# Value units of a conv-MLP kernel: sums formed half a group ahead, and the next group's first block product between a unit's last two

## The chip, the cores and the metric

The kernel runs on one core of a Trainium2 chip (trn2). The metric is the device time in microseconds of one execution; lower is better. Before the change, three runs took 1213.5, 1215.37 and 1215.85 us: a median of 1215.37.

## The reference, cut to what matters

A causal decoder trunk of two layers for 512 tokens of width 1024, all in float32. Layer 0 mixes tokens by sliding-window attention and a short convolution, layer 1 by gated linear attention. After its mixer each layer has the gated MLP with a causal convolution of width 3 that this change is about, and then a per-layer embedding:

```
def _conv_ffn(h, w_up, conv_w, conv_b, w_down):
    u = _causal_depthwise_conv(h @ w_up, conv_w) + conv_b
    gate, up = jnp.split(u, 2, axis=-1)
    return (jax.nn.gelu(gate, approximate=False) * up) @ w_down
...
x = x + _conv_ffn(_rms_norm(x, ffn_norm[i]), ffn_w_up[i], ffn_conv_w[i], ffn_conv_b[i], ffn_w_down[i])
```

`w_up` is 1024 x 5632: 2816 gate columns and 2816 value columns, in 22 blocks of 128 each (`NF` = 22).

## The kernel before, in words

**Precision.** A float32 product is done as three faster fp32r products. Each operand is cut into a rounded part and a remainder: ScalarE copies it to the rounded type (`wh`, line 870 in the `ffn`), VectorE subtracts (`wl`, line 873), and TensorE adds hi x hi, hi x lo and lo x hi (lines 924 to 926, three matmuls of 128 x 256 each per piece). `cut_into` and `cut_blocks` (lines 854 to 876) do one such cut; ScalarE's half is listed in the trace as an ACTIVATE of line 870, VectorE's as a TENSOR_TENSOR of line 873.

**Seven block products.** A pair of column blocks (256 columns) times the 512 tokens is a 2 x 2 block product, and `seven` (lines 928 to 956) does it with seven products of 12 matmuls instead of eight. The tokens' side has the forms e1, o1, o2, s1 to s4; the weights' side has `plain` (blocks as they are), `t13` (two sums of blocks), `t2` (one more combination) and `last` (a remainder of the odd rows, cut late at line 951). The order is: W = plain x e1 in a bank of its own; W copied to the left halves of X and Y (lines 940 and 941); V = t13 x s1 beside W; X left += plain x o1; Y left += t2 x s2; Y left copied to X right (line 950); X right += t13 x s3, copied to Y right (line 953); Y left += last x s4; X right += last x o2. It is a generator: the caller takes it step by step and puts other products between the steps.

**Groups.** `ffn` (from line 960) runs over eleven groups d of a gate pair and the two value blocks that come after it. A gate pair is always done by `seven`. The values are done as full products of 24 matmuls (`value`), but in groups 1 and 4 (`pairs_by_blocks`) by a `Unit` (lines 1062 to 1095), which does a value pair in the same seven products, between the gate's steps. TensorE's order is written out by hand (main loop from line 1195): `first` (the unit's W) comes after the gate's Y left; `second` (V, X left, Y left, then the cut of `last`) after the gate's X right; `third` (X right s3) after the gate's last product; then `begin` for the next group, which for a unit is the next gate's W, and `fourth` (Y left s4, X right o2). The order on the other engines comes from a scheduler, which the code steers with `tc.issue_after(instruction)` and `tc.high_priority(offset)`.

**Sums.** `sum_ahead` (line 1022) has the DMA engines form the sums of weight blocks that make `t13`: one 512 KB transfer from GpSimd's queue (line 1028), and when it has landed two accumulating transfers of 256 KB (line 1030). It is used for the gate pairs of groups 1, 2 and 3, and for the two units. `sum_forms` (line 1034) then cuts them. For a unit (`apart`) it cuts `plain`, cuts the sums into a tile `four` (the trace shows `four<-four` at line 870), forms b11 (line 1042), cuts it as t2 and forms b21 (line 1045). A unit's sums were asked for as early as the scheduler would take them.

**Loads.** Gate weights are loaded by SyncE (line 1108), values too (line 1001), 1 MB each, into two `raw` buffers. A buffer is free when VectorE has done `last`'s remainder. `prepare(d)` (lines 1097 to 1118) issues the sums and loads of group d and the cuts that follow; it is called at the end of group d - 1, with `copied`, that group's copy at line 953.

VectorE and ScalarE also run the convolution taps of every group (lines 978 to 990), the gelu (line 1245) and the product of gate and value (line 1138). In the trace, a matmul whose right operand is listed as `four,wh` is one with the sums of token forms.

Of the kernel before, what the change touches and what calls it, by code (L numbers as in the profile page):

```python
# [19 lines left out]
P = 128  # L20
# [4 lines left out]
DFF = 2816  # L25
# [35 lines left out]
HALVES = (slice(0, S // 2), slice(S // 2, S))  # L61


class Kernel:
# [860 lines left out]
            mm(out, wh, xl, start=False, stop=False, **kw)  # L925
            mm(out, wl, xh, start=False, stop=j == ND // 2 - 1, **kw)  # L926

    def seven(self, od, ws, x, keep=None):


        nc = self.nc
        H = S // 2
        product = self.block_product
        left, right = HALVES
        W = self.pa()
        V = W[:, right]
        X, Y = self.ps(), self.ps()
        plain, t13, t2 = ws
        product(W[:, left], plain, 0, x["e1"], True)
        nc.scalar.copy(X[:, left], W[:, left])  # L940
        nc.scalar.copy(Y[:, left], W[:, left])
        yield
        product(V, t13, 0, x["s1"])
        more = V
        if keep is not None:
            more = keep()
            nc.scalar.copy(more, V)
        product(X[:, left], plain, 1, x["o1"])
        product(Y[:, left], t2, 0, x["s2"])
        yield nc.scalar.copy(X[:, right], Y[:, left])  # L950
        last = self.cut_blocks(od)
        product(X[:, right], t13, 1, x["s3"])
        yield nc.scalar.copy(Y[:, right], X[:, right])
        product(Y[:, left], last, 1, x["s4"])
        product(X[:, right], last, 0, x["o2"])
        yield X, Y, more

    def ffn(self, i, project, next_gain):


        nc, a, tc = self.nc, self.a, self.tc
        gain = self.g_ffn[i]
        wu = a["ffn_w_up"][i].rearrange("(k p) n -> p k n", p=P)
        w0, w1, w2, bb = self.fcv

        mine, other = (("a0", "a1"), ("b0", "b1"))[:: 1 - 2 * i]
        with tc.tile_pool(name=f"ffn{i}", bufs=1) as fp:
# [27 lines left out]
            def load_values(d):  # L995

                c0, c1 = DFF + 256 * d + P, min(DFF + 256 * d + 3 * P, 2 * DFF)
                if d < 0:
                    c0 = DFF
                raw = self.raw(ND, 256)[:, :, : c1 - c0]  # L1000
                nc.sync.dma_start(raw, wu[:, :, c0:c1])
                return raw

            def column(raw, c):
                return self.cut(raw[:, :, c * P : (c + 1) * P], "b", BLOCKS)
# [11 lines left out]
            pairs_by_blocks = (1, 4)  # L1017
            ahead_of = {0: (1, 2), 1: (3,)}
            blocks = a["ffn_w_up"][i].rearrange("(j u p) n -> u p j n", p=P, u=2)
            gate_sums, value_sums, places = {}, {}, {}  # L1020

            def sum_ahead(sums, d, c):
                key = id(sums)
                if key not in places:
                    x = self.four(fp, F32).rearrange("p (h a) b -> p h (a b)", h=2)
                    places[key] = [x[:, h].rearrange("p (j n) -> p j n", n=2 * P) for h in range(2)]
                x = sums[d] = places[key][d % 2 if sums is gate_sums else 0]
                nc.gpsimd.dma_start(x, blocks[0, :, :, c : c + 2 * P])
                for u in range(2):
                    nc.gpsimd.dma_start(  # L1030
                        x[:, :, u * P : (u + 1) * P], blocks[u, :, :, c + P : c + 2 * P], accum_op=ALU.add
                    )

            def sum_forms(raw, both13, apart=False):
                ev, od = self.by_parity(raw)
                if apart:
                    b11, b21, b22 = ev[:, :, :P], od[:, :, :P], od[:, :, P:]
                    plain = self.cut_blocks(raw[:, :, :P])
                    four = self.four(fp)
                    h, l = (four[:, 2 * u : 2 * u + 2].rearrange("p a b -> p (a b)") for u in range(2))  # L1040
                    t13 = self.cut_into(h, l, both13)
                    nc.vector.tensor_tensor(b11, b22, both13[:, :, :P], ALU.add)
                    with tc.high_priority(offset=40):
                        t2 = self.cut_blocks(b11, False)
                    nc.vector.tensor_tensor(b21, b21, b11, ALU.add)
                    return plain, t13, t2
                plain = self.cut_blocks(raw[:, :, :P])
                given = both13 is not None
                if not given:
                    both13 = ev  # L1050
                first, third = both13[:, :, :P], both13[:, :, P:]
                if not given:
                    nc.vector.tensor_tensor(first, ev[:, :, P:], ev[:, :, :P], ALU.add)
                    nc.vector.tensor_tensor(third, od[:, :, P:], ev[:, :, P:], ALU.add)  # L1054
                t13 = self.cut_blocks(both13)
                nc.vector.tensor_tensor(first, od[:, :, P:], first, ALU.add)
                with tc.high_priority(offset=40):
                    t2 = self.cut_blocks(first, False)
                nc.vector.tensor_tensor(od[:, :, :P], od[:, :, :P], first, ALU.add)
                return plain, t13, t2  # L1060

            class Unit:
# [22 lines left out]
                    u.last = self.cut_blocks(u.od)  # L1085

                def third(u):
                    right = HALVES[1]
                    self.block_product(u.X[:, right], u.t13, 1, operands["s3"])
                    nc.scalar.copy(u.Y[:, right], u.X[:, right])  # L1090

                def fourth(u):
                    left, right = HALVES
                    self.block_product(u.Y[:, left], u.last, 1, operands["s4"])
                    self.block_product(u.X[:, right], u.last, 0, operands["o2"])

            def prepare(d, behind=None):

                if d == 0:
                    values.append(load_values(-1))  # L1100
                rv, w0 = values.pop(), None
                if d - 1 not in pairs_by_blocks:
                    with tc.issue_after(behind.ins) if behind else nullcontext():
                        w0 = column(rv, rv.shape[2] // P - 1)
                if d in pairs_by_blocks:
                    sum_ahead(value_sums, d, DFF + 256 * d + P)
                rg = self.raw(ND, 256)
                nc.sync.dma_start(rg, wu[:, :, 256 * d : 256 * d + 256])
                ev, od = self.by_parity(rg)
                ws = sum_forms(rg, gate_sums.get(d))  # L1110
                values.append(load_values(d))
                steps = self.seven(od, ws, operands, self.aside)
                for e in ahead_of.get(d, ()):
                    sum_ahead(gate_sums, e, 256 * e)
                if d not in pairs_by_blocks:
                    return steps, w0, column(values[0], 0)
                rv = values[0]
                return steps, w0, Unit(rv, sum_forms(rv, value_sums[d], True))

            def begin(d, steps, w):  # L1120

# [71 lines left out]
            operands = self.tokens_and_forms(xg, self.forms)  # L1193
            ready = []

            def done(m, ps):
                nc.vector.tensor_tensor(self.xT[m], self.xT[m], ps, ALU.add)
                self.operand(m, gain, mine)

            project(done, lambda: ready.extend(prepare(0)))  # L1200
            steps, w0c, w1c = ready
            with tc.manual_schedule(engines={ET.PE}):
                late = begin(0, steps, w0c)
                close = lambda: None
                for d in range(groups):
# [4 lines left out]
                    unit = w1c if isinstance(w1c, Unit) else None  # L1210
# [17 lines left out]
                    if d + 1 < groups:  # L1228
                        steps, w0c, w1c = prepare(d + 1, copied)
                        if unit:  # L1230
                            unit.third()
                            w0c = unit
                        else:
                            cut = self.rest_cut
                        late = begin(d + 1, steps, w0c)
                    else:
                        split_acts()
# [1174 lines left out]
```

## Time and profile before

| what | value |
|---|---|
| median of three runs | 1215.37 us |
| profiled execution | 1216.1 us |
| its span, first to last instruction | 1214.3 us |
| its mean granted TensorE clock | 0.995 |
| TensorE busy | 1192.9 us, 98% |
| VectorE busy | 1001.8 us, 83% |
| ScalarE busy | 701.5 us, 58% |

The profiled execution's own time is 1.8 us above its span, which is what lies around the first and the last instruction. Waits are written behind a row of the timeline in brackets: the idle time in us ahead of the instruction, and what released it. `PE ... [1.85 <-ACT wh L870]` says that TensorE stood for 1.85 us until ScalarE's rounding of line 870 was done. A row begins with its start (us from the span's start) and its length. In the windows, the column behind the five engines is the granted clock of TensorE.

The two MLPs lie at 178 to 440 us (layer 0) and 803 to 1085 us (layer 1). Their units are in groups 1 and 4: at about 204 to 239 and 273 to 302, and at 830 to 862 and 898 to 925.

### The profile page before, as it was taken

To read this page: it belongs to the slowest core of one execution; us is meant where nothing else is said; L and a number is where in the kernel's file an instruction comes from. 1 tells how busy PE (TensorE), PEld (TensorE's weight loads), DVE (VectorE), ACT (ScalarE), POOL (GpSimd) and SP (SyncE) were. 2 spreads that over 40 slices of the span, in tenths; PEclk is the share of its full clock that TensorE was granted. 3 is DMA by queue.
4 is the path that set the end of the run, shared out by engine and by line. 5 is a ranking of instruction groups with operands and counts; after the bars stand their busy time and mean duration, and the time that the engine had idled before them with its cause. 6 is when DMAs were issued, how large, how long until landed. Compare 5 with 4: busy or idle time off the path is not lost.

```text
span 1214.3 us, 20267 instructions
## 1 busy us (share of the span) xinstructions
PE 1192.9 (98%) x8170; PEld 1080.3 (89%) x8170; DVE 1001.8 (83%) x1603; ACT 701.5 (58%) x1166; POOL 80.0 (7%) x94
## 2 busy tenths in 40 slices
PE   9999999899999999999999999999999999999998
PEld 8887789898999989989988988899999999888887
DVE  6786688698999996789879876687898999988595
ACT  7466556455556654666674655555565556646374
POOL 3600211100000000000100002012000000000000
PEclk9999999899999999999999999999999999999999
DMA  7222553542333343322412215345323242433501
GB/s 220 84 92 70 127 126 100 125 136 70 106 104 107 120 134 100 105 77 80 148 59 67 87 56 134 92 129 159 95 83 127 71 139 75 145 103 96 206 2 70
DMA packets 125074, 128.26 MB, mean 106 GB/s; under 512 B 3336, under 2 KB 118722, under 8 KB 124980
## 3 DMA queue, kind: packets, MB, share of 16 engines
q1 hardware_dynamic: 112144, 115.88, 29.7%
q0 software_dynamic: 12560, 10.91, 5.0%
q8 instruction: 64, 1.05, 0.4%
q14 instruction: 30, 0.25, 0.1%
q10 hardware_dynamic: 276, 0.18, 0.0%
HBM read 124.86 MB, written 2.10 MB: 105 GB/s over the span
## 4 chain that ended last, share of the span: by engine, by line
PE 72%; DVE 12%; DMA 6%; issue 6%; ACT 4%; POOL 1%; ACTq 0%; POOLq 0%; DVEq 0%; SPq 0%
PE ps L177 8%; PE ps L178 8%; PE ps L179 7%; PE ps L193 4%; PE ps L191 4%; DMA four<-in_ffn_w_up_dram 4%; PE ps L200 4%; PE ps L924 4%; PE ps L926 4%; PE ps L925 4%; PE pa L178 3%; PE pa L179 3%; PE pa L177 3%; DVE wl L873 3%; DVE zt L990 2%
## 5 line engine op out<-in xcount | busy, mean ns | idle before, releaser
L153 DVE TENSOR_TENSOR wl<-raw,wh 128x1024 fp32r<-128x1024 f32 (+3 forms) x130 | 149.2, 1150 | 36.3 <-ACT wh L151 33.7
L151 ACT ACTIVATE wh<-raw 128x1024 fp32r<-128x1024 f32 (+4 forms) x134 | 132.5, 991 | 69.2 <-PE ps L178 26.9
L870 ACT ACTIVATE wh<-raw 128x1024 fp32r<-128x1024 f32 x92 | 97.7, 1062 | 116.1 <-DVE raw L1054 42.3
L873 DVE TENSOR_TENSOR wl<-raw,wh 128x1024 fp32r<-128x1024 f32 x92 | 112.6, 1224 | 34.3 <-ACT wh L870 33.2
L990 DVE SCALAR_TENSOR_TENSOR zt<-z,vfa,zt 128x511 f32<-128x511 f32 (+1 forms) x176 | 129.9, 747 | 1.6 <-ACT zt L988 1.1
L988 ACT ACTIVATE zt<-z,vfb 128x512 f32<-128x512 f32 x88 | 70.5, 812 | 31.4 <-DVE z L978 13.9
L179 PE MATMUL pa<-b,wl 128*128 128x256 f32 x288 | 79.7, 277 | 0.1
L179 PE MATMUL pa<-a,wl 128*128 128x256 f32 x288 | 79.6, 276 | 0.0
L177 PE MATMUL pa<-b,wh 128*128 128x256 f32 x288 | 79.5, 276 | 0.0
L178 PE MATMUL pa<-b,wh 128*128 128x256 f32 x288 | 79.5, 276 | 0.0
L177 PE MATMUL pa<-a,wh 128*128 128x256 f32 x288 | 79.5, 276 | 0.0
L178 PE MATMUL pa<-a,wh 128*128 128x256 f32 x288 | 79.5, 276 | 0.0
L191 PE MATMUL ps<-b,wh 128*128 128x512 f32 (+1 forms) x192 | 72.9, 383 | 0.0
L193 PE MATMUL ps<-b,wh 128*128 128x512 f32 (+1 forms) x192 | 72.2, 379 | 0.0
L924 PE MATMUL ps<-four,wh 128*128 128x256 f32 x232 | 64.9, 280 | 1.0 <-ACT ps L950 1.0
L926 PE MATMUL ps<-four,wl 128*128 128x256 f32 x232 | 64.1, 276 | 0.0
L925 PE MATMUL ps<-four,wh 128*128 128x256 f32 x232 | 64.1, 276 | 0.0
L179 PEld LDWEIGHTS pa<-b,wl 128*128 128x128 f32 x288 | 54.1, 188 | 0.3 <-DVE wl L153 0.2
L177 PEld LDWEIGHTS pa<-b,wh 128*128 128x128 f32 x288 | 54.1, 188 | 0.0
L178 PEld LDWEIGHTS pa<-b,wh 128*128 128x128 f32 x288 | 54.1, 188 | 0.0
L177 PEld LDWEIGHTS pa<-a,wh 128*128 128x128 f32 x288 | 54.1, 188 | 0.0
L178 PEld LDWEIGHTS pa<-a,wh 128*128 128x128 f32 x288 | 54.1, 188 | 0.0
(564 smaller groups left out, 3947.2 us busy)
## 6 DMA issues: line engine op xcount, KB each, us to landing
raw<-in_ffn_w_up_dram SPq DMA_DIRECT2D x42, 1024.0 KB, 5.0
raw<-in_ffn_w_down_dram SPq DMA_DIRECT2D x13, 1024.0 KB, 5.2
raw<-in_hy_w_in_dram SPq DMA_DIRECT2D x8, 1024.0 KB, 5.2
raw<-in_gla_w_in_dram SPq DMA_DIRECT2D x8, 1024.0 KB, 5.1
raw<-in_ffn_w_down_dram SPq DMA_DIRECT2D x8, 768.0 KB, 4.9
raw<-in_ple_w_gate_dram SPq DMA_DIRECT2D x6, 1024.0 KB, 5.4
four<-in_ffn_w_up_dram POOLq DMA_DIRECT2D x10, 512.0 KB, 4.6
four<-in_ffn_w_up_dram POOLq DMA_DIRECT2D x20, 256.0 KB, 6.6
```

The source lines that it names most:

```text
L151: nc.scalar.activation(hv, v, AF.Copy)
L153: self.rest_cut = nc.vector.tensor_tensor(lv, v, hv.bitcast(F32), ALU.subtract)
L177: mm(out, lh, rh, start=start, stop=False, **kw)
L178: mm(out, lh, rl, start=False, stop=False, **kw)
L179: mm(out, ll, rh, start=False, stop=stop, **kw)
L191: mm(out, lh, rh, start=first, stop=False, **kw)
L193: end = mm(out, lt, rt, start=False, stop=False, **kw)
L873: nc.vector.tensor_tensor(l, src, h.bitcast(F32), ALU.subtract)
L924: mm(out, wh, xh, start=first and j == 0, stop=False, **kw)
L925: mm(out, wh, xl, start=False, stop=False, **kw)
L926: mm(out, wl, xh, start=False, stop=j == ND // 2 - 1, **kw)
L990: nc.vector.scalar_tensor_tensor(out=y[:, tap:], in0=z[:, : S - tap], scalar=w[:, f : f + 1], in1=y[:, tap:], op0=ALU.mult, op1=ALU.add,)
```

## The change

It has four parts. Line numbers of the changed kernel are one higher than those above from line 928 on, and up to five higher behind line 1110.

1. The sums of a unit are issued after the `copied` instruction of the group before. Their first transfer is issued from ScalarE's queue instead of GpSimd's; the two accumulating ones stay on GpSimd's.
2. The cut of these sums into `t13` is issued after the same instruction.
3. `third` now does X right s3, the copy of X right to Y right, and Y left s4. `fourth` does X right o2 alone. The next gate's W thus stands between the unit's last two products instead of ahead of both.
4. In a unit's group, the gate's `last` cut has a priority that is higher by 100.

```diff
-    def seven(self, od, ws, x, keep=None):
+    def seven(self, od, ws, x, keep=None, sooner=0):
...
-        last = self.cut_blocks(od)
+        with self.tc.high_priority(offset=sooner) if sooner else nullcontext():
+            last = self.cut_blocks(od)
...
-            def sum_ahead(sums, d, c):
+            def sum_ahead(sums, d, c, q=nc.gpsimd):
...
-                nc.gpsimd.dma_start(x, blocks[0, :, :, c : c + 2 * P])
+                q.dma_start(x, blocks[0, :, :, c : c + 2 * P])
...
-            def sum_forms(raw, both13, apart=False):
+            def sum_forms(raw, both13, behind=None):
...
-                    t13 = self.cut_into(h, l, both13)
+                    with tc.issue_after(behind.ins):
+                        t13 = self.cut_into(h, l, both13)
...
                 def third(u):
-                    right = HALVES[1]
+                    left, right = HALVES
                     self.block_product(u.X[:, right], u.t13, 1, operands["s3"])
                     nc.scalar.copy(u.Y[:, right], u.X[:, right])
 
+                    self.block_product(u.Y[:, left], u.last, 1, operands["s4"])
+
                 def fourth(u):
-                    left, right = HALVES
-                    self.block_product(u.Y[:, left], u.last, 1, operands["s4"])
+                    right = HALVES[1]
                     self.block_product(u.X[:, right], u.last, 0, operands["o2"])
...
                 if d in pairs_by_blocks:
-                    sum_ahead(value_sums, d, DFF + 256 * d + P)
+                    with tc.issue_after(behind.ins):
+                        sum_ahead(value_sums, d, DFF + 256 * d + P, nc.scalar)
...
-                steps = self.seven(od, ws, operands, self.aside)
+                unit = d in pairs_by_blocks
+                steps = self.seven(od, ws, operands, self.aside, 100 if unit else 0)
...
-                return steps, w0, Unit(rv, sum_forms(rv, value_sums[d], True))
+                return steps, w0, Unit(rv, sum_forms(rv, value_sums[d], behind))
```

More of the change, by code (lines that the diff above doesn't have):

```diff
@@ L1032, in sum_ahead @@
                     )
-            def sum_forms(raw, both13, apart=False):
+            def sum_forms(raw, both13, behind=None):
                 ev, od = self.by_parity(raw)
-                if apart:
+                if behind:
                     b11, b21, b22 = ev[:, :, :P], od[:, :, :P], od[:, :, P:]
@@ L1111, in prepare @@
                 values.append(load_values(d))
-                steps = self.seven(od, ws, operands, self.aside)
+                unit = d in pairs_by_blocks
+                steps = self.seven(od, ws, operands, self.aside, 100 if unit else 0)
                 for e in ahead_of.get(d, ()):
                     sum_ahead(gate_sums, e, 256 * e)
-                if d not in pairs_by_blocks:
+                if not unit:
                     return steps, w0, column(values[0], 0)
                 rv = values[0]
-                return steps, w0, Unit(rv, sum_forms(rv, value_sums[d], True))
+                return steps, w0, Unit(rv, sum_forms(rv, value_sums[d], behind))
             def begin(d, steps, w):
```

## The prediction

> **What bounds the kernel now.** I read the head of the page first, then TensorE's waits by line, then the timeline of TensorE around the four units (groups 1 and 4 of each layer), and last ScalarE's timeline and the DMA queues there. Page and waits (engine, tile, line, waited for; total us, times, longest):
>
> ```profile
> span 1214.3 us, 20267 instructions
> ...
> PE 1192.9 (98%) x8170; PEld 1080.3 (89%) x8170; DVE 1001.8 (83%) x1603; ACT 701.5 (58%) x1166; POOL 80.0 (7%) x94
> ```
> ```profile
> PE pa L924 <- ACT wh L870: 4.5, 3, 2.4
> PE pa L924 <- ACT ps L941: 4.3, 4, 2.2
> PE pa L926 <- DVE wl L873: 2.8, 5, 0.8
> PE pa L924 <- ACT pa L1090: 2.1, 2, 1.4
> ```
>
> TensorE is the bound. These four rows add up to 13.7 us, and the timeline places nearly all of it around the units:
>
> ```profile
> 206.57 0.28 PE L924 MATMUL pa<-four,wh 128*128 128x256 f32 x1
> ...
> 210.65 0.28 PE L924 MATMUL pa<-a,wh 128*128 128x256 f32 x1
> ...
> 223.87 0.38 PE L924 MATMUL pa<-a,wh 128*128 128x256 f32 x1 [1.85 <-ACT wh L870]
> ...
> 225.13 0.39 PE L926 MATMUL pa<-a,wl 128*128 128x256 f32 x1 [0.76 <-DVE wl L873]
> ...
> 233.09 0.50 PE L924 MATMUL pa<-four,wh 128*128 128x256 f32 x1 [2.17 <-ACT ps L941]
> ...
> 275.65 0.28 PE L924 MATMUL pa<-four,wh 128*128 128x256 f32 x1
> ...
> 281.47 0.38 PE L924 MATMUL ps<-four,wh 128*128 128x256 f32 x1 [0.21 <-ACT ps L950]
> ...
> 291.83 0.39 PE L924 MATMUL pa<-a,wh 128*128 128x256 f32 x1 [0.25 <-ACT wh L870]
> ...
> 293.09 0.38 PE L926 MATMUL pa<-a,wl 128*128 128x256 f32 x1 [0.76 <-DVE wl L873]
> ...
> 295.96 0.38 PE L924 MATMUL pa<-four,wh 128*128 128x256 f32 x1 [1.43 <-ACT pa L1090]
> ...
> 832.33 0.28 PE L924 MATMUL pa<-four,wh 128*128 128x256 f32 x1
> ...
> 850.21 0.39 PE L924 MATMUL pa<-b,wh 128*128 128x256 f32 x1 [2.41 <-ACT wh L870]
> ...
> 851.47 0.58 PE L926 MATMUL pa<-b,wl 128*128 128x256 f32 x1 [0.75 <-DVE wl L873]
> ...
> 858.29 0.38 PE L924 MATMUL pa<-four,wh 128*128 128x256 f32 x1 [1.30 <-ACT ps L941]
> ...
> 899.80 0.28 PE L924 MATMUL pa<-four,wh 128*128 128x256 f32 x1
> ...
> 906.23 0.38 PE L924 MATMUL ps<-four,wh 128*128 128x256 f32 x1 [0.82 <-ACT ps L950]
> ...
> 918.39 0.39 PE L924 MATMUL pa<-four,wh 128*128 128x256 f32 x1 [0.68 <-ACT pa L1090]
> ```
>
> From 206.57 to 210.65 run three products of 12 matmuls: 1.36 us each, 0.113 per matmul. Each wait costs about 0.16 more than its row says, because the next matmul's start is shown 0.16 past the release. Then there is the clock (columns: window, length, busy us of PE, PEld, DVE, ACT, POOL with instructions, granted clock):
>
> ```profile
> 225.20:231.00 5.80, 5.72 (x34) 5.53 (x34) 1.71 (x2) 0.07 (x1) 0.00 (x0) 0.71 0.67 97
> 233.10:237.00 3.90, 3.90 (x20) 3.90 (x21) 3.90 (x7) 2.44 (x3) 0.00 (x0) 0.56 0.00 0
> 850.00:854.20 4.20, 3.23 (x15) 3.03 (x15) 3.06 (x3) 1.38 (x3) 0.00 (x0) 0.62 1.07 169
> ```
>
> 34 matmuls in 5.80 us where 0.113 each asks 3.85: 1.95 lost; 20 in 3.90: 1.6 lost; in the third, less the 0.21 and 0.75 of waiting inside it, 15 in 3.24: 1.5 lost. So what can be won per unit is:
> - layer 0, group 1: 1.85 + 0.76 + 2.17 + 3 x 0.16 + 1.95 + 1.6 = 8.8
> - layer 1, group 1: 2.41 + 0.75 + 1.30 + 0.48 + 1.5 = 6.4
> - layer 0, group 4: 0.21 + 0.25 + 0.76 + 1.43 + 0.64 = 3.3
> - layer 1, group 4: 0.82 + 0.68 + 0.32 = 1.8
>
> Together 20.3 us, 1.7% of the time: the most that the change could bring. Why TensorE waits there is in ScalarE's timeline:
>
> ```profile
> 194.76 1.06 ACT L151 ACTIVATE wh<-raw 128x1024 fp32r<-128x1024 f32 x1
> ...
> 222.76 1.06 ACT L870 ACTIVATE wh<-raw 128x1024 fp32r<-128x1024 f32 x1 [3.99 <-DMA raw<-in_ffn_w_up_dram]
> ...
> 230.93 1.06 ACT L870 ACTIVATE four<-four 128x1024 fp32r<-128x1024 f32 x1 [5.89 <-DMA four<-in_ffn_w_up_dram]
> ...
> 232.71 0.33 ACT L941 COPY ps<-pa 128x256 f32<-128x256 f32 x1
> ...
> 263.94 1.06 ACT L151 ACTIVATE wh<-raw 128x1024 fp32r<-128x1024 f32 x1
> ...
> 820.14 1.06 ACT L151 ACTIVATE wh<-raw 128x1024 fp32r<-128x1024 f32 x1
> ...
> 888.72 1.06 ACT L151 ACTIVATE wh<-raw 128x1024 fp32r<-128x1024 f32 x1
> ```
>
> At 222.76 the next gate's rounding waits for its load (this makes the 1.85). At 230.93 the rounding of group 4's value sums, scheduled three groups early, blocks ScalarE for 5.89 us, with the copy L941 that the V product needs behind it (this makes the 2.17).
>
> **The change part by part.** No TensorE work is added or removed. The prices of the sums are:
>
> ```profile
> 174.07 0.78 POOL L1028 DMA_DIRECT2D four<-in_ffn_w_up_dram  x1 [25.10 <-DVE four L110]
> 178.60 2.57 POOL L1030 DMA_DIRECT2D four<-in_ffn_w_up_dram  x2 [3.75 <-DMA four<-in_ffn_w_up_dram]
> ```
> ```profile
> four<-in_ffn_w_up_dram POOLq DMA_DIRECT2D x20, 256.0 KB, 6.6
> ```
> ```profile
> four<-in_ffn_w_up_dram POOLq DMA_DIRECT2D x2, 256.0 KB, 5.5
> ```
> ```profile
> four<-in_ffn_w_up_dram POOLq DMA_DIRECT2D x2, 256.0 KB, 10.6
> ```
>
> (From issue to landing, medians: of all twenty accumulating transfers; of the pair issued at 178.60, with the queues quiet; and of the pair issued at 219.09, the group 4 sums that the rounding at 230.93 waited for, with a third sum and a 1 MB load in flight.)
>
> (1) *Sums later.* The first transfer of a unit's sums now stands on ScalarE's queue behind the previous group's copy of Y's right half, in the built order one place behind the L151 rounding. Its issue is thus at 194.76 + 1.06 = 195.8, and at 265.0, 821.2 and 889.8. The accumulating pair starts 4.5 us later (174.07 to 178.60), the second of them about 0.8 after the first (the issue of 0.78), and lands 5.5 to 10.6 after that. So T, from issue to sums, lies between 10.8 and 15.9. With the values' load in flight but no third sum I stay near the quiet end and the median 6.6 (11.9), and take T = 11.6. The sums are there at 207.4, 276.6, 832.8, 901.4. The issue's own time on ScalarE (SyncE's queue shows nothing dearer than the 0.78) falls where ScalarE has slack. GpSimd's gate sums for group 3 now queue behind the unit's pair, some 4 us later; they are read only two groups on: nothing.
>
> (2) *Rounding behind them.* In the built order of ScalarE the rounding of these sums stands ahead of the copies L940 and L941 of the unit's own group, and the V product waits for L941. Behind the waiting rounding therefore stand t2's rounding or a tap, both copies, and TensorE. From T: 0.96 + 0.6 + 0.7 until V may start, 2.2 together (the two copies and the rounding are of the kind at 230.93 to 233.09, which took 2.16). V comes at 209.6, 278.8, 835.0 and 903.6 where it was at 206.57, 275.65, 832.33 and 899.80: 3.0, 3.2, 2.7 and 3.8 late. VectorE's half of the same rounding blocks VectorE just as long, with 3 to 4 us of taps and remainders piled up behind it. The gate's third copy L950 needs these (through t2's rounding in ScalarE's order), so the product X right, four products behind V (V + 5.44), is another 1.2 to 1.5 late. In all 4.4 per unit, and where 0.37 and 0.98 were waited for L950 before, that is inside it. In exchange the far-early rounding at 230.93 is gone, and with it its wait at the next V.
>
> (3) *The order of products.* Y left now follows X right at once and needs the copy of X right into Y right. Last matmul start to copy 0.3, copy 0.36, then 0.05: 0.6 stands open in every unit, and TensorE no longer has the next W to do in it. In ScalarE's order that copy stands behind the next gate's plain rounding, so behind its load. If that load is late, Y left waits and not W. The load starts when the unit's group frees its buffer, 4.4 later by (2), less up to 1.3 by (4); TensorE is 4.4 late too. So the load is hidden better by the 1.3 at most, and by the 1.36 of Y left's place less the copy. I take 0.6 to 1.5 at this place: 1.3 in layer 0, group 1, where the load was slowest, 0.7 else.
>
> (4) *`sooner`.* The gate's last remainder on VectorE passes two taps of 0.66 each in the built order. It frees the raw buffer up to 1.3 us sooner; costs nothing elsewhere, as the taps have a group's time.
>
> The sum, new losses less old ones: layer 0, group 1: 4.4 + 1.3 - 8.8 = -3.1. Layer 1, group 1: 4.4 + 0.7 - 6.4 = -1.3. Layer 0, group 4: 4.4 + 0.7 - 3.3 = +1.8. Layer 1, group 4, the latest (3.8 instead of about 3): 5.3 + 0.7 - 1.8 = +4.2. Total +1.6. The profiled execution took 1216.1 us (span 1214.3), so 1217.7; the median of the three runs, 1215.37, lies 0.7 below it: **1217.0**. Each us in T moves all four units, so 4 us in the sum: T of 10.8 gives 1213.8, T of 13 gives 1222.6, T of 15.9 would give 1234.
>
> The clock: before, waits of 1.85 and 0.76 in one stretch, and of 2.17, were followed by windows of 0.71 and 0.56. The waits of 2.7 to 3.8 ahead of V should thus lower it too, 1.6 each. I take this as covered, since X right has to wait for L950 anyway (1.2 to 1.5 late); uncovered it is up to 4 x 1.6. [...]
>
> **The rivals.**
> - *The sums come sooner (faster).* For it: the first transfer is alone on ScalarE's queue, and group 4's sums leave the crowd at 219 to 231. With the pair as at 178.60 and a first transfer 0.6 quicker than GpSimd's, T is 10.2, and the four units win 1.4 each: 1217 - 5.6 = 1211.4. Against it: the values' own 1 MB load starts within 1.5 us of the sums. [...] The limit, with all that the change names hidden, is 1215.4 - 20.3 = 1195.
> - *The sums come later (slower).* One mechanism: the pair shares the DMA engines with the two 1 MB loads of the same group, and ScalarE and VectorE stand still behind it, four times. For it: the rounding at 230.93 stood 5.89 for just such a pair, and the row at 222.76 has a 1 MB load that was itself waited for 3.99. From T = 11.8 on the change costs over 0.2%; at T = 13, a quarter of the way from 11.9 to 15.9, it gives 1222.6, and with half the uncovered clock 1225.
> - *It doesn't do what it says (slower).* Y left, behind the copy that stands behind the load, waits as long as W did (1.85 and 2.41, not 1.3 and 0.7), in every unit: 3 us more, 1220.
>
> **How the numbers follow.** Forecast as worked out 0.38; sooner 0.22; later 0.30; Y left 0.07; the limit 0.03. A measurement of this kernel can tell about 0.2%, 2.4 us, from no change. The forecast lies 1.6 up, so its share is 0.32 within, 0.04 above, 0.02 below. Faster 0.22 + 0.03 + 0.02 = 0.27; within 0.32; slower 0.30 + 0.07 + 0.04 = 0.41. The range reaches from 1210 (T of 10) to 1225; outside are the limit, some 0.05 of the sooner case and 0.1 of the later one.
>
> **What would show it.** Step 1: pair issued about 4.5 after 195.8, landed at 207 to 208. Step 2: TensorE's row at V (L924 <- ACT ps L941) with 2.5 to 4 us, four times, and ScalarE's rounding four<-four waiting 3 us or more for DMA in each unit; the wait of 5.89 at 230.93 gone. Step 3: Y left <- ACT pa of Y's copy in all four units, 0.5 to 1.5. It is wrong if the rounding finds its sums landed, if V's waits are under 2, or if TensorE's waits sum to far less than 14 us.

## The result, and the profile after

The changed kernel takes 1223.86 us (median of four runs, 1223.01 to 1226.54), the kernel before 1214.43 (four runs, 1213.09 to 1215.85): a ratio of 1.0081, 95% interval 1.006 to 1.0102. It is slower by 0.8%, some 9.4 us. The profiled execution is the slowest of the four (1226.54); its span is 1224.8 us and its mean clock 0.994.

TensorE's waits in the changed kernel, by line (engine, tile, line, waited for; total us, times, longest us):

```profile
PE pa L924 <- ACT ps L941: 14.0, 9, 4.0
PE pa L924 <- ACT pa L1092: 6.0, 4, 3.2
PE ps L924 <- ACT ps L950: 1.9, 2, 1.1
PE pa L926 <- DVE wl L873: 1.5, 4, 0.9
```

The wait of W for its weights (`wh` L870, 4.5 us before) is gone altogether, and the waits for the weights' remainders have halved. In their place V now waits 14.0 us for its copy L941 (4.3 before; 9.6 of the 14.0 are in the units' own groups, nearly all the rest in groups 6 and 7), and Y left 6.0 us for the copy of X right, L1092 (2.1 before, as L1090). The timeline of TensorE shows where:

```profile
209.27 0.38 PE L924 MATMUL pa<-four,wh 128*128 128x256 f32 x1 [1.83 <-ACT ps L941]
...
215.94 0.39 PE L924 MATMUL ps<-four,wh 128*128 128x256 f32 x1 [0.84 <-ACT ps L950]
...
229.35 0.58 PE L924 MATMUL pa<-four,wh 128*128 128x256 f32 x1 [3.24 <-ACT pa L1092]
...
279.05 0.44 PE L924 MATMUL pa<-four,wh 128*128 128x256 f32 x1 [1.93 <-ACT ps L941]
...
296.67 0.38 PE L924 MATMUL pa<-four,wh 128*128 128x256 f32 x1 [0.50 <-ACT pa L1092]
...
319.96 0.38 PE L926 MATMUL pa<-a,wl 128*128 128x256 f32 x1 [0.94 <-DVE wl L873]
...
324.18 0.39 PE L924 MATMUL pa<-four,wh 128*128 128x256 f32 x1 [1.42 <-ACT ps L941]
...
346.35 0.38 PE L924 MATMUL pa<-four,wh 128*128 128x256 f32 x1 [0.70 <-ACT ps L941]
...
841.99 0.39 PE L924 MATMUL pa<-four,wh 128*128 128x256 f32 x1 [4.03 <-ACT ps L941]
...
860.75 0.39 PE L924 MATMUL pa<-four,wh 128*128 128x256 f32 x1 [1.72 <-ACT pa L1092]
...
907.73 0.38 PE L924 MATMUL pa<-four,wh 128*128 128x256 f32 x1 [1.82 <-ACT ps L941]
...
914.55 0.38 PE L924 MATMUL ps<-four,wh 128*128 128x256 f32 x1 [1.05 <-ACT ps L950]
...
925.06 0.38 PE L924 MATMUL pa<-four,wh 128*128 128x256 f32 x1 [0.50 <-ACT pa L1092]
```

Each unit waits at V and at Y left, and two of the four also at X right (215.94 and 914.55). The rows at 319.96 and 324.18 lie in group 6, two groups behind a unit, and the one at 346.35 in group 7. ScalarE in the first unit's group, ACTq being an issue on its DMA queue:

```profile
194.86 0.39 ACTq L1029 DMA_DIRECT2D four<-in_ffn_w_up_dram  x1
...
207.10 1.06 ACT L870 ACTIVATE four<-four 128x1024 fp32r<-128x1024 f32 x1 [5.28 <-DMA four<-in_ffn_w_up_dram]
208.06 0.61 ACT L870 ACTIVATE t<-four 128x512 fp32r<-128x512 f32 x1
208.58 0.36 ACT L940 COPY ps<-pa 128x256 f32<-128x256 f32 x1
208.89 0.33 ACT L941 COPY ps<-pa 128x256 f32<-128x256 f32 x1
...
226.33 1.06 ACT L870 ACTIVATE wh<-raw 128x1024 fp32r<-128x1024 f32 x1 [1.96 <-DMA raw<-in_ffn_w_up_dram]
227.29 1.04 ACT L870 ACTIVATE wh<-four 128x1024 fp32r<-128x1024 f32 x1
228.24 0.80 ACT L989 ACTIVATE zt<-z,vfb 128x512 f32<-128x512 f32 x1
228.94 0.36 ACT L1092 COPY pa<-pa 128x256 f32<-128x256 f32 x1
```

Both of the big waits can be read off here. At 207.10 the rounding of the unit's sums has stood 5.28 us for its transfers, and the two copies that V needs run only behind it. At 226.33 the next gate's rounding has waited for its load, two more roundings or taps follow, and only then, at 228.94, the copy that Y left needs.

Where the time goes: I compared the start of the same matmul in both traces (after less before). The two profiled executions are 10.4 us apart (1226.54 and 1216.1), a little more than the medians. The difference is +0.70 us ahead of layer 0's MLP already; it arises in the first 7 us, varies between 0 and +1.0 in the runs below, and so is no effect of the change. Then:

| stretch | forecast, us | measured, us |
|---|---|---|
| layer 0, unit of group 1 | -3.1 | +0.6 |
| layer 0, unit of group 4 | +1.8 | +0.8 |
| layer 0, groups 5 to 7 | 0 | +3.4 |
| layer 1, unit of group 1 | -1.3 | +0.9 |
| layer 1, unit of group 4 | +4.2 | +1.7 |
| layer 1, groups 5 to 7 | 0 | +2.1 |

### The profile page after: what moved, and what is told of

The parts are those of the page before. It is cut to its first block, busy times and chain, and to the rows that moved or that the text cites. A ratio compares the mean times of both kernels' runs of the same rounds, so it can differ in the third digit from the quotient of the medians.

```text
span 1224.8 us, 20264 instructions
## 1 busy us (share of the span) xinstructions
PE 1194.5 (98%) x8170; PEld 1082.2 (88%) x8170; DVE 1002.1 (82%) x1603; ACT 700.9 (57%) x1166; POOL 77.0 (6%) x90
## 4 chain that ended last, share of the span: by engine, by line
PE 55%; DVE 17%; DMA 5%; ACT 4%; issue 2%; POOL 0%; ACTq 0%; POOLq 0%; DVEq 0%; SPq 0%
PE ps L177 5%; PE ps L178 5%; PE ps L179 5%; DVE zt L991 4%; PE ps L193 4%; PE ps L191 4%; DVE wl L873 4%; PE ps L200 3%; PE ps L924 3%; DMA four<-in_ffn_w_up_dram 3%; PE ps L926 3%; PE ps L925 3%; PE pa L179 3%; PE pa L177 3%; PE pa L178 3%
## 5 line engine op out<-in xcount | busy, mean ns | idle before, releaser
L151 ACT ACTIVATE wh<-raw 128x1024 fp32r<-128x1024 f32 (+4 forms) x134 | 132.5, 992 | 71.0 <-PE ps L178 28.7
L870 ACT ACTIVATE wh<-raw 128x1024 fp32r<-128x1024 f32 x92 | 97.7, 1062 | 118.4 <-DVE raw L1056 42.2
L989 ACT ACTIVATE zt<-z,vfb 128x512 f32<-128x512 f32 x88 | 70.3, 808 | 23.8 <-DVE z L986 12.8
L924 PE MATMUL pa<-four,wh 128*128 128x256 f32 x132 | 39.6, 300 | 20.0 <-ACT ps L941 14.0
```

The lines of the kernel that those rows point to most:

```text
L151: nc.scalar.activation(hv, v, AF.Copy)
L924: mm(out, wh, xh, start=first and j == 0, stop=False, **kw)
```

## The experiments

Theory A: what costs is that the sums land late while their rounding stands on ScalarE ahead of the copies that V needs. Rival B: the new order of products costs, by Y left's wait. Rival C: ScalarE's queue itself is dear. The ratios are to the kernel before on the same chip, with their 95% intervals.

### e1_sums_early

```diff
-                    with tc.issue_after(behind.ins):
-                        sum_ahead(value_sums, d, DFF + 256 * d + P, nc.scalar)
+                    sum_ahead(value_sums, d, DFF + 256 * d + P)
```

> The changed kernel with its first part undone: a unit's sums are asked for as early as before, all three transfers on GpSimd's queue; their rounding still stands behind the copy of the group before, and the order of products and the priority stay. Theory A, the sums come too late: TensorE's four waits at V (1.83, 1.93, 4.03, 1.82 us in the changed kernel) and the two at X right (0.84, 1.05) go, and so do the waits of groups 5 and 6 that VectorE's lag makes; about 14 us less, 1208 to 1212, under the kernel before. Theory B, the order of products: the waits of Y left (3.24, 0.50, 1.72, 0.50, 6.0 together) stay and the time stays above 1219.

Measured: 1215.04 us, ratio 1.0013 (1.0005 to 1.0022). The four waits at V fall to at most 0.83 us and groups 5 to 7 take as long as in the kernel before, so some 8 us of the loss hang on the late sums, as theory A has it. But the time is 3 us above A's range. The rest is in two waits of X right (2.71 and 2.88 us, in the units of group 1), four of Y left (5.5 us together), and these rows of its TensorE and ScalarE:

```profile
PE pa L924 <- ACT pa L1086: 5.6, 2, 2.9
```
```profile
294.95 0.38 PE L924 MATMUL pa<-four,wh 128*128 128x256 f32 x1 [3.10 <-ACT pa L1092]
```
```profile
288.62 1.07 ACT L870 ACTIVATE wh<-raw 128x1024 fp32r<-128x1024 f32 x1 [2.60 <-DMA raw<-in_ffn_w_up_dram]
...
293.57 1.06 ACT L870 ACTIVATE wh<-raw 128x1024 fp32r<-128x1024 f32 x1 [2.86 <-DVE raw L1056]
294.53 0.37 ACT L1092 COPY pa<-pa 128x256 f32<-128x256 f32 x1
```

Both of the unit's copies (L1086 and L1092) stand behind roundings of the next gate that wait for a load, and then for VectorE. So B has a part too, and it is a matter of ScalarE's order again.

### e2_order_alone

```diff
                 def third(u):
...
+                    self.block_product(u.Y[:, left], u.last, 1, operands["s4"])
...
                 def fourth(u):
-                    self.block_product(u.Y[:, left], u.last, 1, operands["s4"])
```

> The kernel before with the third part alone: Y left ahead of the next gate's W. Theory A: no loss by it, 1213 to 1217, Y left waiting for its copy about as long as W waited for its load before (1.85 and 2.41 in the units of group 1). Theory B: the copy behind the load costs more than W's wait did, 1219 or more.

Measured: 1217.92 us, 1.0046 (1.0029 to 1.0062): between the two. In the profiled execution, at 1223.67 us the slowest of the six, Y left's waits for its copy sum to 12.9 us, far more than W waited before (4.5); the median one probably has less of it. The new order alone is a loss in the kernel before.

```profile
PE pa L924 <- ACT pa L1091: 12.9, 4, 5.0
```

### e3_order_undone

```diff
-                    self.block_product(u.Y[:, left], u.last, 1, operands["s4"])
...
                 def fourth(u):
...
+                    self.block_product(u.Y[:, left], u.last, 1, operands["s4"])
```

> The changed kernel with the third part undone: W ahead of Y left as before, sums and rounding late, priority kept. Theory A: it keeps the loss, 1221 or more, V waiting 1.8 to 4 us four times. Theory B: it falls back to 1214 to 1217.

Measured: 1225.26 us, 1.0103 (1.009 to 1.0116). Theory A: the loss stays whole without the new order, and with it V's waits and those of group 6. B is not the cause of the 9.4 us.

```profile
PE pa L924 <- ACT ps L941: 12.6, 7, 4.0
```

### e4_gpsimd_queue

```diff
-                        sum_ahead(value_sums, d, DFF + 256 * d + P, nc.scalar)
+                        sum_ahead(value_sums, d, DFF + 256 * d + P)
```

> The changed kernel with the first transfer of a unit's sums back on GpSimd's queue, still issued behind the copy of the group before. Theory A: the queue matters little; the sums come 0 to 1 us later, 1223 to 1228. Rival C, ScalarE's queue is what is slow, or its issue holds ScalarE up: 1219 or less, V's waits at least 1 us shorter each.

Measured: 1215.03 us, 1.0015 (1.0002 to 1.0027). By its numbers this speaks for C, but the row on GpSimd's queue says that the kernel wasn't what I took it for:

```profile
174.41 0.78 POOL L1029 DMA_DIRECT2D four<-in_ffn_w_up_dram  x1 [25.07 <-DVE four L110]
```

The transfer starts at 174.41, as early as in the kernel before, and 20 us ahead of the copy behind which it is "issued after". In this run `issue_after` gave no more than a place in an order: on GpSimd's queue the transfer did not wait for the copy on ScalarE. On ScalarE's own queue, in the changed kernel, the place held it until 194.86. So this run in effect repeats e1_sums_early and says nothing of the queue.

### e5_scalar_early

```diff
-                    with tc.issue_after(behind.ins):
-                        sum_ahead(value_sums, d, DFF + 256 * d + P, nc.scalar)
+                    sum_ahead(value_sums, d, DFF + 256 * d + P, nc.scalar)
```

> The changed kernel with the sums' first transfer on ScalarE's queue, but not held behind the copy of the group before. Theory A, lateness: in group 1 the issue stands some 10 us sooner in ScalarE's order, the rounding finds its sums landed or nearly so, and the waits at V shrink to under 1 us; 1214 to 1219 (in group 4 the issue itself may stand in ScalarE's way, as it must wait until the first unit's sums have been read). Rival C, ScalarE's queue itself is what costs: 1221 or more.

Measured: 1216.94 us, 1.003 (1.0018 to 1.0043). ScalarE's queue, but issued at 184.65 instead of 194.86: the waits at V are at most 1.0 us. That is well under C's 1221. It lies 0.17% above e1_sums_early, with intervals that overlap a little, so up to some 2 us for the queue at this early place are not ruled out.

### e6_gpsimd_late

```diff
...
+                if behind:
+                    with tc.issue_after(behind.ins):
+                        nc.scalar.copy(x[:, 0, :1], self.copied_to[:, :1])
+                    q = nc.gpsimd
                 q.dma_start(x, blocks[0, :, :, c : c + 2 * P])
...
```

> The changed kernel with the sums' first transfer on GpSimd's queue and truly late: ScalarE writes one column of the sums' tile behind the copy of the group before (0.2 us more on ScalarE, four times), and the transfer must wait for that write. Theory A: as late, so as slow, V waits 1.8 to 4 us, 1223 to 1229. Rival C: 1218 or less.

Measured: 1238.17 us, 1.0193 (1.0174 to 1.0211): slower still than A had it. On GpSimd's queue, behind ScalarE's write, the transfer leaves at 199.47, and the first unit's sums take until 213.81:

```profile
199.47 0.82 POOL L1034 DMA_DIRECT2D four<-in_ffn_w_up_dram  x1 [4.45 <-ACT four L1032]
```
```profile
213.81 1.06 ACT L870 ACTIVATE four<-four 128x1024 fp32r<-128x1024 f32 x1 [8.89 <-DMA four<-in_ffn_w_up_dram]
```
```profile
PE pa L924 <- ACT ps L941: 31.8, 6, 8.8
```

So the run is not as late as the changed kernel but 4.6 us later (199.47 against 194.86), and that is most of the 6.7 us by which its sums are rounded later (213.81 against 207.10). From issue to rounding it takes 14.3, 12.8, 12.2 and 11.8 us in the four units, a mean of 12.8 against 12.3 in the changed kernel. The later the sums, the longer V waits, on a queue that is not ScalarE's; C falls as the main cause. Which queue is the better at the same late place is not shown.

### e7_round_behind_copies

The sums are as late as in the changed kernel. Only their rounding, and what follows from it, is formed behind the copy that V waits for:

```diff
-        nc.scalar.copy(Y[:, left], W[:, left])
-        yield
+        yield nc.scalar.copy(Y[:, left], W[:, left])
...
-                    with tc.issue_after(behind.ins):
-                        t13 = self.cut_into(h, l, both13)
...
+                    def rest(behind):
+                        with tc.issue_after(behind.ins):
+                            t13 = self.cut_into(h, l, both13)
...
-                    next(steps)
+                    self.opened = next(steps)
...
                         late = begin(d + 1, steps, w0c)
+                        if isinstance(w1c, Unit):
+                            w1c.t13, w1c.t2 = w1c.rest(self.opened)
```

> The changed kernel with the sums as late as there, but their rounding behind the copy of the unit's own W (the one that V waits for) instead of ahead of it. Theory A in its narrow form, the loss is that the rounding that waits for the sums holds up the two copies behind it on ScalarE: V's four waits go, X right's and the lag of VectorE with them mostly (VectorE still waits for the rounding), 1212 to 1218. If the sums are simply too late for the unit itself, the unit's own V takes over the waits (about 2 us each) and the time stays at 1221 or more.

Measured: 1216.93 us, 1.0015 (1.0 to 1.003). Its transfers are issued at 194.33 (194.86 in the changed kernel), and the rounding now starts here:

```profile
206.90 1.06 ACT L870 ACTIVATE four<-four 128x1024 fp32r<-128x1024 f32 x1 [0.68 <-DMA four<-in_ffn_w_up_dram]
```
```profile
PE pa L924 <- ACT pa L1095: 6.1, 4, 1.9
PE pa L924 <- ACT pa L1089: 4.6, 1, 4.6
PE pa L924 <- ACT ps L941: 2.8, 4, 1.4
```

The waits for L941 fall from 14.0 to 2.8 us, and 7 to 8 us of the 9.4 are back (7 by the medians, 8 by the ratios), with the sums half a us sooner at most. This is the narrow form of theory A: not the late sums, but what stood behind their rounding. What is left are the copies of the unit (L1095 and L1089 here, L1092 and L1086 in the changed kernel).

### e8_copies_first

e1_sums_early, and the next gate's first rounding is placed behind the unit's last copy. For that, `prepare` as a whole is called behind `third`:

```diff
+                        if unit:
+                            unit.third()
-                        steps, w0c, w1c = prepare(d + 1, copied)
+                        steps, w0c, w1c = prepare(d + 1, copied, unit.copied if unit else None)
...
-                plain = self.cut_blocks(raw[:, :, :P])
+                with tc.issue_after(copy.ins) if copy else nullcontext():
+                    plain = self.cut_blocks(raw[:, :, :P])
```

> Sums early (as in e1_sums_early), and the next gate's first rounding held behind the unit's copy of X right into Y right, so that neither this copy nor the one before it stands behind a load on ScalarE. If those copies' queueing is what eats the gain of the new order, the waits at X right (2.71, 2.88 us) and Y left (3.10, 1.40, 0.50, 0.50) fall to 0.5 to 0.6 for Y left and nothing for X right, W waits for its load for what is left of it, and the time is 1207 to 1212, below the kernel before. If the loads are late anyhow, W's wait takes it all back: 1213 to 1217.

Measured: 1210.42 us, 0.9968 (0.9956 to 0.998): faster than both kernels.

```profile
PE pa L924 <- ACT ps L941: 5.2, 9, 0.9
PE pa L926 <- DVE wl L873: 3.0, 8, 0.5
PE pa L924 <- ACT pa L1093: 2.0, 4, 0.5
```

Y left waits 0.50 in each unit, the bare round trip of the copy, and W doesn't wait for its load at all (no row `wh` L870).

### e9_early_behind_first

The edits of e7_round_behind_copies and e8_copies_first together, sums early.

> Sums early, the next gate's first rounding behind the unit's copy (as in e8_copies_first), and the sums' rounding behind the copies of the unit's own group (as in e7_round_behind_copies). If the 0.94 us that V still waits in the units of group 4 comes of the sums' rounding and its companions standing ahead of V's copy, it goes: 1208 to 1210. If it is VectorE's lag, it stays: 1210 to 1212.

Measured: 1209.04 us, 0.9959 (0.9944 to 0.9974). V's 0.94 in the units of group 4 is gone, but X right takes over 0.80 of it: a us at most, not clear from e8_copies_first by the intervals.

### e10_old_order

e8_copies_first with W again ahead of Y left (the edit of e3_order_undone).

> The kernel of e8_copies_first with the third part undone: the next gate's W again ahead of the unit's Y left and X right. It has the sums early, their rounding behind the copy of the group before, the priority, and the next gate's rounding behind the unit's copy. If the new order of products is worth anything where ScalarE's order serves it, this one waits for loads at W, 1 to 2 us in the units of group 1 and more by the copy ahead of the rounding, 1212 to 1216; if the order is worth nothing, 1209 to 1211 as in e8_copies_first.

Measured: 1216.08 us, 1.0018 (1.0005 to 1.0031). W waits 6.5 us for its rounding, 1.47 to 2.09 in each unit, and 0.76 for its remainder.

```profile
PE pa L924 <- ACT wh L870: 6.5, 4, 2.1
```

So with ScalarE's order made for the new products, the new order is worth 0.5% (1.0018 against 0.9968), against a loss of 0.46% when put alone into the kernel before. This ScalarE order doesn't suit the old products, for which W needs the rounding that is now held back. Against the kernel before, which has both the old order and a ScalarE order of its own, e8_copies_first gains 0.3%.

### e11_late_all_behind

The changed kernel, late sums and all, with the edits of e7_round_behind_copies and e8_copies_first.

> The changed kernel with its late sums as they are, their rounding behind the copies of the unit's own group (e7_round_behind_copies) and the next gate's rounding behind the unit's copy (e8_copies_first). If sums that come half a group ahead are early enough once nothing that TensorE needs stands behind them on ScalarE, 1209 to 1213, as good as with early sums; if lateness costs by itself, 1215 or more, with waits in the unit's own V or X right.

Measured: 1208.98 us, 0.9956 (0.9939 to 0.9972), 1.2% below the changed kernel by the two ratios. Its sums are issued at 194.63 (194.86 in the changed kernel), and the rounding finds them landed:

```profile
206.15 0.36 ACT L941 COPY ps<-pa 128x256 f32<-128x256 f32 x1
206.55 1.06 ACT L870 ACTIVATE four<-four 128x1024 fp32r<-128x1024 f32 x1
```
```profile
PE pa L924 <- ACT ps L941: 4.4, 9, 0.8
PE pa L924 <- ACT pa L1096: 2.0, 4, 0.5
```

So the late sums and the new order of products do no harm, and the order pays, if two things on ScalarE stand the other way round. By the medians this kernel and e9_early_behind_first are the fastest here; their intervals overlap with that of e8_copies_first, so late sums are as good as early ones, and no gain of lateness itself is shown.

### e12_no_priority

```diff
-                steps = self.seven(od, ws, operands, self.aside, 100 if unit else 0)
+                steps = self.seven(od, ws, operands, self.aside, 0)
```

> The changed kernel without the raised priority of the gate's last cut (fourth part undone). By the prediction it frees the raw buffer up to 1.3 us sooner in each unit, so that without it Y left waits for its load by up to that much more in the units of group 1 (3.24 and 1.72 us in the changed kernel), and nothing else moves: 1223 to 1227. If the priority harms, by putting the remainder ahead of taps that VectorE then owes to the groups behind, 1222 or less.

Measured: 1225.54 us, 1.0101 (1.0085 to 1.0116), overlapping with the changed kernel's 1.0081 (1.006 to 1.0102). Y left's waits are 3.36 and 1.53 against 3.24 and 1.72: the 1.3 us that the priority was to save don't show. The two ratios differ by 0.2%, less than their intervals can tell, so what it is worth stays open.

## Why the prediction was right, and where its terms were wrong

The forecast was 1217.0 us, slightly slower, with 1223.86 inside its range but near the end. The mechanism was named: V behind the rounding of the sums, and Y left behind the load (steps 2 and 3). Four of its sizes were wrong, and one step was missing. That the time still lies in the range is in part luck. The four units cost 4.0 us together where the sum had 1.6, and another 5.5 came from groups that it put at nothing; the upper half of the range was made for a longer T, and T is not what filled it.

By its own signs the prediction is half borne out. The 5.89 at 230.93 is gone, and each of the four roundings waits for its transfers, but 3 us or more in two of them only (5.28, 2.84, 5.80, 2.44). V's row is under 2 us in three units (1.83, 1.93, 1.82), which was named as a sign of being wrong, and 4.03 in the fourth. Y left's rows are 3.24, 0.50, 1.72 and 0.50, two of them above the 0.5 to 1.5.

**Step 1, T from issue to sums.** Forecast 11.6 us. Measured from issue to rounding: 12.2 (194.86 to 207.10), 11.7, 13.7 and 11.6, a mean of 12.3. The lower bound of 10.8 was misread. The 5.5 is the median of a pair that landed 4.8 and 6.3 us after issue, and the sums need the second: with 6.3, the quiet T is 11.6. The rival's 10.2 was out of reach by the same row. On the other hand the issue is sooner than I had it. It came within 0.3 us of the start of the copy that it follows, ahead of it in three units of four, and ahead of the rounding L151 in all of them, although it stands behind both in ScalarE's order. Less what TensorE lagged by then (0.7, 1.3, 5.5 and some 6 us), the issue was 1.3 to 2.2 us sooner than forecast. In three units this outweighs T, and the sums came 1 to 2 us sooner than forecast; in layer 1, group 1, with its T of 13.7, they came about 0.8 later, and there V waited its 4.03.

**Step 2, V.** From the sums to V I had 2.2 us; measured 2.17 (207.10 to 209.27), and 2.35, 2.87 and 2.35 in the others. V's wait and X right's together, counted with 0.16 each, came to 3.0, 2.1, 4.2 and 3.2 us in the four units, against 4.4 for three of them and 5.3. The step was right, its size too big, by little in one unit and by 1.4 to 2.3 us in the others. (The 0.16 per wait holds, but not for the reason given. V at 209.27 starts 0.05 behind the end of its copy; idle time is counted from the end of the matmul before, whose row is 0.28 long, while without a wait the next starts after 0.113.) That the rounding's place is the cause, not only named beside it, is shown by e7_round_behind_copies (14.0 us of waits for L941 down to 2.8 with the sums as late). The rows at 207.10 to 208.89 show it in one unit: two copies of 0.36 and 0.33 us, of a product whose last matmul ended at 206.08, run only behind a rounding that waited 5.28 us.

**Step 3, Y left.** I took 1.3 us in layer 0, group 1, and 0.7 else. Measured: 3.4, 0.7, 1.9 and 0.7 with the 0.16. The first is the rival "it doesn't do what it says": the load was issued at 217.94 and took 8.4 us. Of the others two are the bare 0.5 of the round trip, and the 1.9 is the load again. e8_copies_first and e11_late_all_behind show, with early and with late sums, that this wait is one of ScalarE's order: 0.50 in all four units.

**The clock.** I counted the slow clock of before as won (1.95 + 1.6 + 1.5 us) and the new one as covered by X right's wait. It wasn't. Two windows of the changed kernel (columns as before):

```profile
229.35:235.00 5.65, 5.65 (x27) 5.65 (x28) 3.55 (x6) 0.75 (x2) 0.00 (x0) 0.51 0.00 0
```
```profile
841.90:847.00 5.10, 5.01 (x29) 5.01 (x30) 5.10 (x8) 1.45 (x3) 0.78 (x1) 0.67 0.32 106
```

27 matmuls at 0.113 us are 3.05, so 2.6 us lost behind Y left's wait of 3.24; 29 in 5.10 are 1.8 lost behind V's 4.03; a third stretch, 20 matmuls in 3.95 us from 279.05 (its row is shown in the last section), 1.7. In all 6.1, a us more than before. By the windows of 0.71 and 0.56 I expected a lower clock behind all four V's; it came behind two of them (0.57 from 279.05, 0.67 from 841.90), and not behind 209.27 and 907.73 (1.00 in both). In layer 0, group 1, this and Y left turn the forecast -3.1 into +0.6; in layer 1, group 1, V's long wait and the clock make +0.9 of -1.3.

**The missing step: VectorE behind the unit.** I had VectorE's standing time end with the unit. But VectorE is full in the plain group behind a unit: busy for 21.66 of the 22.00 us from 302 to 324, as in the kernel before for 21.68 of those from 298 to 320. So what it is behind TensorE at the end of the unit it still owes two groups on. The waits of VectorE for the sums' rounding, first in the kernel before, then in the changed one:

```profile
DVE four L873 <- ACT four L870: 9.0, 2, 5.1
```
```profile
DVE four L873 <- ACT four L870: 13.5, 4, 5.1
```

and ScalarE in group 6 of the changed kernel:

```profile
322.53 1.06 ACT L870 ACTIVATE wh<-raw 128x1024 fp32r<-128x1024 f32 x1 [3.44 <-DVE raw L1056]
323.49 0.37 ACT L940 COPY ps<-pa 128x256 f32<-128x256 f32 x1
323.79 0.33 ACT L941 COPY ps<-pa 128x256 f32<-128x256 f32 x1
```

ScalarE waits for VectorE's form of the weights, the copies for V stand behind that rounding once more, and TensorE waits 0.94 and 1.42 us in a group that the change doesn't touch, and 0.70 in the one behind it. Groups 5 to 7 lose 3.4 us in layer 0 and 2.1 in layer 1 by this, more than half of the loss.

What brings it on is less simple than "late sums". The new order doesn't: e3_order_undone, without it, loses 3.4 and 2.7 us in the same stretches, e1_sums_early 0.0 and -0.2. But neither do late sums or VectorE's standing by themselves. In e6_gpsimd_late, where the sums are latest and VectorE stands longest for them (23.4 us), the stretches lose 0.3 and -0.5; and in e8_copies_first, with early sums and no such wait, they lose 1.6 and 2.5. A reading that fits all of these is that TensorE loses there whenever it leaves a unit sooner than VectorE can follow. In the changed kernel VectorE stood longer than TensorE; in e6_gpsimd_late TensorE stood as well, 6 to 9 us at each V; in e8_copies_first TensorE was quicker through the unit and VectorE had the same work. This is read from the traces; no run changed VectorE's work alone.

**Step 4, the priority.** No gain of it was seen (e12_no_priority), and no harm; what it is worth stays open.

**The rivals.** "The sums come later" had the right sign and nearly the right time (1222.6 at T = 13), but T was 12.3, and the clock and VectorE's lag made the rest. "The sums come sooner" failed: T did not come down to 10.2. That its first transfer would be 0.6 us quicker than GpSimd's was my estimate, with no row of the kernel before behind it. It may well be quicker on ScalarE's queue (3.4 and 3.6 us for the first units of e5_scalar_early, 4.0 and 4.2 from GpSimd's in e1_sums_early), but the pair behind it took 6.6 to 8.9 us from its first issue to its last landing, 7.1 in the quiet row at 178.60. "It doesn't do what it says" came true in one unit of four, with 3.24 us at Y left.

## What to carry to other kernels

- An instruction that waits for a transfer is placed by what stands behind it on its engine, not by when its own result is needed. Here moving two such roundings behind a few short copies made 1.2% (0.9956 against 1.0081): the same change is a loss of 0.8% without it.
- A new order of work on the busiest engine shows its worth only when the helping engine's order follows it: the same two swapped products cost 0.46% alone, and gained 0.5% where the copies came first.
- When a second engine is nearly as full as the first, what it is behind at the end of one stage can be paid for some stages later. Look for the loss, or for a part of a gain that is given back, behind the stage that was changed, too: here 5.5 us of the loss, and 1.6 and 2.5 us of the gain in e8_copies_first.

## What the runs showed of the hardware

The clock in two windows of the changed kernel, each right behind a wait at V (columns as before):

```profile
209.27:214.00 4.73, 4.73 (x40) 4.73 (x41) 4.73 (x8) 2.97 (x4) 0.78 (x1) 1.00 0.25 74
...
279.05:283.00 3.95, 3.95 (x20) 3.95 (x21) 3.95 (x6) 1.58 (x2) 0.00 (x0) 0.57 0.00 0
```

- The granted clock did not follow the length of the wait alone. Behind 1.93 us of waiting (V at 279.05) it was 0.57, behind 1.83 (V at 209.27) it stayed at 1.00; in e1_sums_early it stayed at 1.00 behind 3.10 (Y left at 294.95). What else decides it is not shown.
- In two runs whose waits at V are at most 0.9 us (e8_copies_first, e11_late_all_behind) the mean granted clock is 1.000, against 0.994 in the changed kernel with waits of up to 4.03 there.
- A transfer issued from ScalarE's queue left before the engine had begun an instruction that stands ahead of it: ACTq at 194.86, the copy ahead of it in the order started at 195.16, and the rounding L151 between the two at 195.47. A place in ScalarE's order held a transfer back (194.86, against 184.65 without it in e5_scalar_early), but in these rows not until the instruction ahead of it is done.
- A float32 matmul of 128 x 128 x 256 took longer than three fp32r matmuls of that shape. In layer 1's attention of the kernel before, two of them, listed as two records each, run from 683.61 to 684.47, 0.43 us each; three fp32r matmuls at 0.113 (the products from 206.57 on) are 0.34.

```profile
683.61 1.02 PE L2239 MATMUL pa<-vt,sc 128*128 128x256 f32 x4
684.47 0.59 PE L2241 MATMUL pa<-st,F 128*128 128x256 f32 x2
```
